# Two small attention products with the high and low parts of one operand side by side

## The chip, the cores and the metric

The kernel runs on one core of one Trainium2 chip, in one launch. The metric is the device time of an execution in microseconds (us), as a median over executions. Lower is better.

## What is computed

A trunk of two layers (`DEPTH = 2`) works on one sequence of 256 positions with 1024 features. A layer is: a gated feed-forward block, attention, a second feed-forward block, and a gated addition of a per-layer embedding. Attention has three branches from one normalised input: a differential attention (branch a), a sparse attention with compressed, selected and windowed keys (branch b) and a sliding-window attention (branch c). The two places that the change touches are these, cut from the reference:

```python
# branch a, diff_attention: 4 heads, 128 values each
attn = pr[:, 0] - lam * pr[:, 1]
o = jnp.einsum('bhqk,bkhe->bqhe', attn, v)            # "values"
o = rms_norm(o, subln_g) * (1.0 - lam_init)
# branch b, nsa_attention: scores against 15 compressed keys per group
s_c = jnp.einsum('bqgrd,bngd->bgrqn', qi, k_cmp) * scale
s_c = s_c + grouped_head_bias(bias_table, dist_c, B_GROUPS, B_REP)
p_c = masked_softmax(s_c, dist_c >= 0)
```

All inputs and outputs are 32-bit floats.

## The kernel before, in words

A matmul on TensorE (PE) takes a stationary operand, which a weight load (PEld) puts in place, and a moving operand that streams through; in this kernel each matmul has its own load. To keep the accuracy of 32-bit floats, each operand is split in two tiles of the type fp32r: a high part (`hi`, made by ScalarE, ACT) and a low part (`lo`, the difference, made by VectorE, DVE). `split` at L225 does it. A product is then three matmuls that add up in one PSUM bank: high times high, high times low, low times high. `mul3` (L234) issues them at L235, L236 and L237. Where `mul3` is called with a stationary pair (xh, xl) and a moving pair (wh, wl), the first two matmuls have the same stationary operand and two moving operands.

The big products (`product`, L305) stream weights from DRAM in pieces of 128x1024 through four `raw` buffers, which ACT (L228) and DVE (L223) split into six pairs of `wh` and `wl`. Names in the profile: `ff` and `fo` are the feed-forward products, `A`, `Ck`, `Cq`, `Bk`, `Bv`, `Bq` the projections of attention, `gate` and `br` the gates and the branch products, `wo` the output product, `pp` and `pg` the embedding's products.

The attention of the three branches runs beside the projections and gates, as side programs (Python generators) that `Flow` steps as the big products go on: `attend_a` from A2 on, `attend_c` from Bk on, `attend_b` after branch a, and `compressed` with `attend_cmp` in a lane of its own. The scheduler of the framework then sets the final order of every engine from dependencies, priorities and a simulated timeline, so the order on each engine is fixed when the kernel is built and each engine works through its own in that order.

Branch a. `attend_a` works on units (m, t): m is a pair of heads, t a block of 128 query rows, four units in a layer. `first` makes the scores `s` (L537, matmuls of 64 rows of the array, two halves of the array in alternation, 12 to a unit) and the softmax. `second` turns the probabilities by transposes (`pt`, L243), splits them (`pT`), and at L626 to L631 multiplies them with the values: the bank `ya` gets, for each head x of the pair and each key block k, a `mul3` whose stationary operands are the probabilities' parts and whose moving operands are 128 columns of the values' high part and low part, `va[0][:, 0, k, hd]` and `va[0][:, 1, k, hd]`. Units with t = 0 have one key block, units with t = 1 have two: 2 x 2 x (1 + 2) = 12 calls in a layer, 24 in all. Then ACT squares `ya` with a sum (L636, twice), DVE (L637) and GpSimd (POOL, L638) make the norm's factor, DVE scales `ya` into `yn` (L639), and PE transposes `yn` (`yt`).

Branch b's compressed keys. `attend_cmp(t)` (L806) forms the scores `sc` of 128 query rows against the compressed keys `kc`: four head pairs j, each a `mul3` with the queries' parts as stationary and 32 columns of `kc`'s high and low part as moving operands (16 calls in all). DVE adds the bias `cbias` (L814), and a softmax and a transpose (`pct`) follow. `own` (L836) later reads the turned result `pcT`.

The bank of `ya` has the tag `y` with one buffer, which `yb` and `yc` use too; the SBUF tiles of tag `stage` have four buffers, shared by the projections' copies, `own`, `rows`, and the norm's squares.

Of the kernel before, what the change touches and what calls it, by code (L numbers as in the profile page):

```python
# [13 lines left out]
AF = mybir.ActivationFunctionType  # L14
ALU = mybir.AluOpType
# [171 lines left out]
def trunk(ctx: ExitStack, tc: tile.TileContext, a: dict, out: bass.AP, index: list):  # L187
    nc = tc.nc
# [7 lines left out]
    def bank(tag, bufs, name):  # L196
        return psum.tile([128, 512], F32, tag=tag, bufs=bufs, name=name)
# [11 lines left out]
    def tp_bank(name):  # L209
        return bank("tp", 3, name)  # L210

    def y_bank(name):
        return bank("y", 1, name)
# [5 lines left out]
    def stage(name="stage"):  # L219
        return base.tile([128, 512], F32, tag="stage", bufs=4, name=name)  # L220
# [13 lines left out]
    def mul3(ps, xh, xl, wh, wl, start, stop):  # L234
        nc.tensor.matmul(ps, xh, wh, start=start, stop=False)  # L235
        nc.tensor.matmul(ps, xh, wl, start=False, stop=False)  # L236
        nc.tensor.matmul(ps, xl, wh, start=False, stop=stop)  # L237
# [266 lines left out]
    def attention(i, norm, after):  # L504
# [21 lines left out]
        def scores(name, q, qb, t, key):  # L526

            ps = [psum.tile([128, 2, 256], F32, tag="s", bufs=2, name=name) for _ in range(2)]
            for m in range(2):
                for x, y in ((0, 0), (0, 1), (1, 0)):  # L530
                    for par in range(2):
                        r = slice(64 * par, 64 * par + 64)
                        kk = key(y, r, m)
                        o = ps[par][:, m, :math.prod(kk.shape[1:])]
                        if len(kk.shape) == 3:
                            o = o.rearrange("p (s n) -> p s n", s=kk.shape[1])
                        nc.tensor.matmul(o, q[r, x, qb[m], t * 128:(t + 1) * 128], kk, start=x + y == 0, stop=x == 1)  # L537
            return ps
# [14 lines left out]
        def turned(blocks):  # L553

            n = len(blocks)
            ps = tp_bank("pt")
            transposes(ps, blocks)
            T = pool.tile([128, 2, 4, 128], F32R, tag="pT", bufs=3, name="pT")
            split(T[:, 0, :n], T[:, 1, :n], ps[:, :n * 128].rearrange("p (j q) -> p j q", q=128))
            return T  # L560
# [11 lines left out]
        def band(first):  # L572
            b = pool.tile([128, 4, 256], F32, tag="band", bufs=2, name="band")
            read_band(b, first)
            return b
# [5 lines left out]
        qk, va, yA = [None] * 2, [None], [None] * NT  # L581
# [16 lines left out]
        def attend_a():  # L598
            bnd = band(0)

            def first(u):
                m, t = u
                nk = 128 * (t + 1)
                s = scores("s", qk[m], [0, 1], t, lambda x, r, k: qk[m][r, x, 2 + k, :nk])
                yield
                p = pool.tile([128, 4, 256], F32, tag="p", bufs=3, name="p")
                st = None
                for st in softmax([p[:, j, :nk] for j in range(4)], [s[j // 2][:, j % 2, :nk] for j in range(4)],
                                  [back(bnd[:, 2 * m + j % 2], nk) for j in range(4)]):
                    yield  # L610
                nc.vector.reciprocal(st[:, 8:12], st[:, 4:8])
                nc.vector.tensor_scalar(st[:, 10:12], st[:, 10:12], nlam[:, i:i + 1], None, op0=ALU.mult)
                for x in range(2):
                    nc.vector.tensor_scalar(p[:, 2 + x, :nk], p[:, 2 + x, :nk], st[:, 10 + x:11 + x], None, op0=ALU.mult)
                    nc.vector.scalar_tensor_tensor(p[:, x, :nk], p[:, x, :nk], st[:, 8 + x:9 + x], p[:, 2 + x, :nk],
                                                   op0=ALU.mult, op1=ALU.add)
                yield
                return p

            def second(u, p):  # L620
                m, t = u
                T = []
                for k in range(t + 1):
                    T.append(turned([p[:, x, k * 128:(k + 1) * 128] for x in range(2)]))
                    yield
                y_ps = y_bank("ya")[:, :256]  # L626
                for x in range(2):
                    o, hd = slice(x * 128, x * 128 + 128), slice((2 * m + x) * 128, (2 * m + x + 1) * 128)
                    for k in range(t + 1):
                        mul3(y_ps[:, o], T[k][:, 0, x, :], T[k][:, 1, x, :], va[0][:, 0, k, hd], va[0][:, 1, k, hd], k == 0, k == t)  # L630
                    yield  # L631
                y = pool.tile([128, 256], F32, tag="yt", bufs=2, name="yn")
                st = pool.tile([128, 32], F32, tag="st", bufs=4, name="st")
                for x in range(2):
                    o = slice(x * 128, x * 128 + 128)
                    nc.scalar.activation(y[:, o], y_ps[:, o], AF.Square, accum_out=st[:, x:x + 1])  # L636
                nc.vector.tensor_scalar(st[:, 2:4], st[:, 0:2], 1.0 / 128, EPS, op0=ALU.mult, op1=ALU.add)  # L637
                nc.gpsimd.tensor_tensor(st[:, 4:6], st[:, 2:4], mhalf[:, :2], op=ALU.pow)  # L638
                nc.vector.tensor_tensor(y.rearrange("p (h e) -> p h e", h=2), y_ps.rearrange("p (h e) -> p h e", h=2),  # L639
                                        st[:, 4:6, None].to_broadcast([128, 2, 128]), op=ALU.mult)  # L640
                yield
                if m == 0:
                    yA[t] = y_tile("yA")
                ps = tp_bank("yt")
                transposes(ps, [y[:, x * 128:x * 128 + 128] for x in range(2)])
                split(yA[t][:, 0, 2 * m:2 * m + 2], yA[t][:, 1, 2 * m:2 * m + 2],
                      ps[:, :256].rearrange("p (k q) -> p k q", k=2), sg[:, i:i + 1])
                yield

            yield from pipelined([(m, t) for m in range(2) for t in range(NT)], first, second)  # L650


        kB, qB, vB, half, sig = [None], [None], [None], [None], [None] * NT
# [54 lines left out]
        kc, vc, c_sb = [None], [None], [None]  # L708
# [96 lines left out]

        def attend_cmp(t):  # L806
            s_ps = tp_bank("sc")
            for j in range(4):
                mul3(s_ps[:, 32 * j:32 * j + 32], qB[0][:, 0, j, t * 128:(t + 1) * 128], qB[0][:, 1, j, t * 128:(t + 1) * 128],
                     kc[0][:, 0, j // 2], kc[0][:, 1, j // 2], True, True)  # L810
            yield
            p = pool.tile([128, 8, 16], F32, tag="pc", bufs=2, name="pc")
            st = pool.tile([128, 32], F32, tag="st", bufs=4, name="st")
            nc.vector.tensor_tensor(p, s_ps[:, :128].rearrange("p (h n) -> p h n", h=8), cbias[:, t], op=ALU.add)  # L814
            nc.vector.tensor_reduce(st[:, 0:8], p, axis=AX.X, op=ALU.max)
            nc.vector.tensor_tensor(p, p, st[:, 0:8, None].to_broadcast([128, 8, 16]), op=ALU.subtract)
            nc.scalar.activation(p, p, AF.Exp)
            yield
            nc.vector.tensor_reduce(st[:, 8:16], p, axis=AX.X, op=ALU.add)
            nc.vector.reciprocal(st[:, 8:16], st[:, 8:16])  # L820
            nc.vector.tensor_tensor(st[:, 0:8].rearrange("p (g a b) -> p g a b", g=2, a=2),
                                    st[:, 8:16].rearrange("p (g a b) -> p g a b", g=2, a=2),
                                    sig[t][:, 0:8].rearrange("p (g b a) -> p g a b", g=2, a=2), op=ALU.mult)
            nc.vector.tensor_tensor(p, p, st[:, 0:8, None].to_broadcast([128, 8, 16]), op=ALU.mult)
            nc.vector.tensor_tensor(p, p, cmask[:, None, t, :].to_broadcast([128, 8, 16]), op=ALU.mult)
            yield
            ps = tp_bank("pct")
            transposes(ps, [p.rearrange("p h n -> p (h n)")])
            pcT[t] = pool.tile([128, 128], F32, tag="pcT", bufs=2, name="pcT")
            nc.scalar.activation(pcT[t], ps[:, :128], AF.Copy)  # L830
            yield
# [257 lines left out]
    h = base.tile([128, NT, D], F32, name="h")  # L1089
# [8 lines left out]
    cbias = base.tile([128, NT, 8, 16], F32, name="cbias")  # L1098
# [10 lines left out]
    def back(b, n, step=1):  # L1109

        return bass.AP(tensor=b.tensor, offset=b.offset + step * (n - 1), ap=list(b.ap)[:-1] + [[-step, n]])
# [65 lines left out]
    for i in range(DEPTH):  # L1177
        n = norms[4 * i:4 * i + 5]
# [68 lines left out]
```

## Time and profile before

| | |
|---|---|
| runs | 1345.94, 1347.99, 1346.43 us |
| median | 1346.43 us |
| the profiled execution's own time | 1346.13 us |
| span of the profiled execution | 1344.3 us, 18242 instructions |
| granted TensorE clock, mean | 0.999 |

| engine | busy us | share of the span | instructions |
|---|---|---|---|
| PE, matmuls | 1326.3 | 99% | 6414 |
| PEld, weight loads | 1093.2 | 81% | 6414 |
| DVE | 945.9 | 70% | 1795 |
| ACT | 783.0 | 58% | 1382 |
| POOL | 20.4 | 2% | 36 |

How to read it: the profile is one execution, and times count from its first instruction. A matmul's row tells when it starts and how long it takes from its start to its modelled end; matmuls overlap, so what one costs in a dense stream is the step from its start to the start of the next one, not its duration. An attention layer takes from about 190 to 470 us and from about 853 to 1133 us.

### The profile page before, as it was taken

How to read it: one execution, taken by the hardware profiler on the slowest of the kernel's cores; microseconds unless marked ns; L12 is line 12 of the kernel's file. 1: busy time of each engine (PE TensorE's matmuls, PEld its weight loads, DVE VectorE, ACT ScalarE, POOL GpSimd, SP SyncE). 2: the span in 40 equal slices, each digit the busy share in tenths (PEclk: the TensorE clock that was granted, in tenths of full speed). 3: DMA queues.
4: the chain of work that ended last, by engine and by line, in shares of the span. 5: the costliest groups of instructions: out<-in, count | busy, mean ns of one | idle time of the engine just before them, and what ended most of it. 6: DMA issues, size and time to landing. Idle time of an engine off the chain costs nothing.

```text
span 1344.3 us, 18242 instructions
## 1 busy us (share of the span) xinstructions
PE 1326.3 (99%) x6414; PEld 1093.2 (81%) x6414; DVE 945.9 (70%) x1795; ACT 783.0 (58%) x1382; POOL 20.4 (2%) x36
## 2 busy tenths in 40 slices
PE   9999999999999999999999999999999999999997
PEld 7778888887887788888888888888888878888886
DVE  6677566768978767665776766577697886767565
ACT  7555455668756555544755545566696656555454
POOL 0000000000000000000000000000000000000000
PEclk9999999999999999999999999999999999999999
DMA  8887665455742578675567875744556425877562
GB/s 302 214 270 220 206 207 187 141 165 168 229 153 79 188 186 237 208 219 184 188 199 216 224 209 186 243 152 162 167 174 207 152 78 177 242 222 214 189 209 78
DMA packets 121993, 257.14 MB, mean 191 GB/s; under 512 B 56944, under 2 KB 62500, under 8 KB 121902
## 3 DMA queue, kind: packets, MB, share of 16 engines
q1 hardware_dynamic: 121150, 254.34, 61.1%
q0 software_dynamic: 320, 1.08, 0.3%
q8 instruction: 50, 0.82, 0.3%
q10 hardware_dynamic: 432, 0.56, 0.1%
q14 instruction: 41, 0.34, 0.1%
HBM read 243.33 MB, written 1.08 MB: 182 GB/s over the span
## 4 chain that ended last, share of the span: by engine, by line
PE 91%; DVE 4%; DMA 2%; ACT 1%; issue 1%; SPq 0%; POOLq 0%; POOL 0%; DVEq 0%; ACTq 0%
PE ff L236 11%; PE ff L237 11%; PE ff L235 11%; PE fo L235 6%; PE fo L236 6%; PE fo L237 6%; PE gate L235 3%; PE gate L237 3%; PE gate L236 3%; PE s L537 2%; PE A L235 2%; PE A L236 2%; PE A L237 2%; DVE wl L223 2%; PE br L236 1%; PE br L235 1%
## 5 line engine op out<-in xcount | busy, mean ns | idle before, releaser
L223 DVE TENSOR_TENSOR wl<-raw,wh 128x1024 fp32r<-128x1024 f32 (+1 forms) x448 | 539.4, 1213 | 174.2 <-ACT wh L228 166.8
L228 ACT ACTIVATE wh<-raw 128x1024 fp32r<-128x1024 f32 (+1 forms) x448 | 468.3, 1050 | 229.0 <-PE fo L237 85.4
L236 PE MATMUL ff<-wl,nT 128*128 128x512 f32 x704 | 273.8, 391 | 1.6 <-DVE wl L223 1.5
L237 PE MATMUL ff<-wh,nT 128*128 128x512 f32 x704 | 272.8, 390 | 0.0
L235 PE MATMUL ff<-wh,nT 128*128 128x512 f32 x704 | 270.9, 391 | 0.3 <-ACT wh L228 0.3
L236 PEld LDWEIGHTS ff<-wl,nT 128*128 128x128 f32 x704 | 132.3, 188 | 30.9 <-DVE wl L223 3.9
L235 PEld LDWEIGHTS ff<-wh,nT 128*128 128x128 f32 x704 | 132.3, 188 | 29.5 <-ACT wh L228 2.1
L237 PEld LDWEIGHTS ff<-wh,nT 128*128 128x128 f32 x704 | 132.3, 188 | 27.3
L236 PE MATMUL fo<-wl,gT 128*128 128x512 f32 x352 | 134.2, 392 | 0.0
L237 PE MATMUL fo<-wh,gT 128*128 128x512 f32 x352 | 133.7, 389 | 0.0
L235 PE MATMUL fo<-wh,gT 128*128 128x512 f32 x352 | 132.5, 389 | 0.0
L474 ACT ACTIVATE act<-ff,stats 128x256 f32<-128x256 f32 x88 | 41.4, 472 | 85.9 <-PE ff L237 85.7
L475 DVE TENSOR_TENSOR gated<-act,ff 128x256 f32<-128x256 f32 x88 | 36.6, 417 | 60.1 <-ACT act L474 60.1
L235 PEld LDWEIGHTS fo<-wh,gT 128*128 128x128 f32 x352 | 66.1, 188 | 13.8
L237 PEld LDWEIGHTS fo<-wh,gT 128*128 128x128 f32 x352 | 66.1, 188 | 13.4
L236 PEld LDWEIGHTS fo<-wl,gT 128*128 128x128 f32 x352 | 66.1, 188 | 13.3
L235 PE MATMUL gate<-wh,nT 128*128 128x512 f32 x192 | 76.3, 399 | 0.0
L237 PE MATMUL gate<-wh,nT 128*128 128x512 f32 x192 | 76.1, 396 | 0.0
L236 PE MATMUL gate<-wl,nT 128*128 128x512 f32 x192 | 75.9, 395 | 0.0
L228 ACT ACTIVATE gT<-whole 128x512 fp32r<-128x512 f32 (+1 forms) x48 | 28.4, 591 | 64.3 <-DVE whole L448 64.2
L548 ACT ACTIVATE p<-p,st 128x128 f32<-128x128 f32 (+1 forms) x128 | 56.8, 445 | 2.9 <-DVE st L546 2.2
L448 DVE COPY whole<-flip 128x512 uint16<-128x512 uint16 (+1 forms) x96 | 38.2, 433 | 14.5 <-DMA flip<-cut 13.9
(301 smaller groups left out, 1997.6 us busy)
## 6 DMA issues: line engine op xcount, KB each, us to landing
raw<-in_wst SPq DMA_DIRECT2D x438, 512.0 KB, 4.4
band<-table SPq DMA_DIRECT2D x10, 512.0 KB, 5.1
raw<-in_wbv SPq DMA_DIRECT2D x4, 420.0 KB, 3.0
flip<-cut SPq DMA_TRANSPOSE x96, 4.1
xt<-in_xt SPq DMA_DIRECT2D x4, 256.0 KB, 5.3
raw<-in_wst SPq DMA_DIRECT2D x4, 256.0 KB, 4.9
h<-in_x SPq DMA_DIRECT2D x2, 512.0 KB, 7.6
band<-table POOLq DMA_DIRECT2D x2, 512.0 KB, 6.9
```

What stands on the lines that cost most here:

```text
L223: nc.vector.tensor_tensor(o, x, y, op=ALU.subtract)
L228: nc.scalar.activation(hi, src, AF.Copy)
L235: nc.tensor.matmul(ps, xh, wh, start=start, stop=False)
L236: nc.tensor.matmul(ps, xh, wl, start=False, stop=False)
L237: nc.tensor.matmul(ps, xl, wh, start=False, stop=stop)
L448: tc.keep_in_program_order(nc.vector.tensor_copy(halves(whole)[:, :128 * m, w], flip[:, w, :m].rearrange("p a b -> p (a b)")))
L474: nc.scalar.activation(act, ps[:, :256], AF.Silu, scale=norm.r(t))
L475: nc.vector.tensor_tensor(held[t][:, 256 * (f % 2):256 * (f % 2) + 256], act, ps[:, 256:], op=ALU.mult)
L537: nc.tensor.matmul(o, q[r, x, qb[m], t * 128:(t + 1) * 128], kk, start=x + y == 0, stop=x == 1)
L548: nc.scalar.activation(p[j], p[j], AF.Exp, bias=st[:, j:j + 1], scale=-1.0, accum_out=st[:, n + j:n + j + 1])
```

## The change

In branch a the first two matmuls of each call become one: the moving operand is 256 columns, the values' high part and, beside it, their low part, and the bank `ya` holds for each head 128 columns of the product with the high part and 128 of the product with the low part. The third matmul (low probabilities, high values) adds to the first half. The two halves are added afterwards: ACT copies the low halves to a `stage` tile (128x256), DVE adds the high halves to it (128x256), and the squares and the scaling that follow read this tile in SBUF in place of the bank.

In `attend_cmp` the same is done with 2 x 32 columns of `kc`; here DVE adds the second half to the scores in one more 128x128 addition.

```diff
-                y_ps = y_bank("ya")[:, :256]
+                y_ps = y_bank("ya").rearrange("p (x v e) -> p x v e", x=2, v=2)
                 for x in range(2):
-                    o, hd = slice(x * 128, x * 128 + 128), slice((2 * m + x) * 128, (2 * m + x + 1) * 128)
+                    hd = slice((2 * m + x) * 128, (2 * m + x + 1) * 128)
                     for k in range(t + 1):
-                        mul3(y_ps[:, o], T[k][:, 0, x, :], T[k][:, 1, x, :], va[0][:, 0, k, hd], va[0][:, 1, k, hd], k == 0, k == t)
+                        nc.tensor.matmul(y_ps[:, x], T[k][:, 0, x, :], va[0][:, :, k, hd], start=k == 0, stop=False)
+                        nc.tensor.matmul(y_ps[:, x, 0], T[k][:, 1, x, :], va[0][:, 0, k, hd], start=False, stop=k == t)
                     yield
                 y = pool.tile([128, 256], F32, tag="yt", bufs=2, name="yn")
+                ys = stage("ya")
                 st = pool.tile([128, 32], F32, tag="st", bufs=4, name="st")
+                nc.scalar.activation(ys[:, 256:].rearrange("p (x e) -> p x e", x=2), y_ps[:, :, 1], AF.Copy)
+                nc.vector.tensor_tensor(ys[:, :256].rearrange("p (x e) -> p x e", x=2), y_ps[:, :, 0],
+                                        ys[:, 256:].rearrange("p (x e) -> p x e", x=2), op=ALU.add)
+                y_ps = ys[:, :256]
...
             s_ps = tp_bank("sc")
+            s_ps = s_ps[:, :256].rearrange("p (x n) -> p x n", x=2)
             for j in range(4):
-                mul3(s_ps[:, 32 * j:32 * j + 32], qB[0][:, 0, j, t * 128:(t + 1) * 128], qB[0][:, 1, j, t * 128:(t + 1) * 128],
-                     kc[0][:, 0, j // 2], kc[0][:, 1, j // 2], True, True)
+                q = [qB[0][:, x, j, t * 128:(t + 1) * 128] for x in range(2)]
+                nc.tensor.matmul(s_ps[:, :, 32 * j:32 * j + 32], q[0], kc[0][:, :, j // 2], start=True, stop=False)
+                nc.tensor.matmul(s_ps[:, 0, 32 * j:32 * j + 32], q[1], kc[0][:, 0, j // 2], start=False, stop=True)
...
-            nc.vector.tensor_tensor(p, s_ps[:, :128].rearrange("p (h n) -> p h n", h=8), cbias[:, t], op=ALU.add)
+            nc.vector.tensor_tensor(p, s_ps[:, 0].rearrange("p (h n) -> p h n", h=8), cbias[:, t], op=ALU.add)
+            nc.vector.tensor_tensor(p, p, s_ps[:, 1].rearrange("p (h n) -> p h n", h=8), op=ALU.add)
```

Since the framework's scheduler sets the order from a simulated timeline, the order of the other attention work moves too. The feed-forward blocks and the output product keep theirs. Counted over the whole program, PE has 40 matmuls less, ACT eight instructions more and DVE twelve. The score matmuls `s` (L537) stand in unbroken runs between other matmuls; there are 54 such runs before and 42 after (27 in each layer before; 22 and 20 after).

First place, PE at the first unit of branch a in the first layer, inside the projection Cq. Before:

```order
L537 MATMUL s<-qkA_1868 128x128 x6
L243 MATMUL qt<-ident,stage 128x128 x2
L235 MATMUL ya<-va,pT 128x128
L236 MATMUL ya<-va,pT 128x128
L537 MATMUL s<-qkA_1868 128x128 x2
L237 MATMUL ya<-va,pT 128x128
L235 MATMUL ya<-va,pT 128x128
L236 MATMUL ya<-va,pT 128x128
L237 MATMUL ya<-va,pT 128x128
L537 MATMUL s<-qkA_1868 128x128 x4
```

After the change, at the same place:

```order
L537 MATMUL s<-qkA_1868 128x128 x6
L243 MATMUL qt<-ident,stage 128x128 x2
L630 MATMUL ya<-va,pT 128x256
L537 MATMUL s<-qkA_1868 128x128 x3
L631 MATMUL ya<-va,pT 128x128
L630 MATMUL ya<-va,pT 128x256
L631 MATMUL ya<-va,pT 128x128
L537 MATMUL s<-qkA_1868 128x128 x3
```

Six matmuls of 128 columns became two of 256 and two of 128; the scores around them are cut at another point.

Second place, PE in the gates of branch a in the first layer, where branch c's scores and values (`yc`) are put between. Before:

```order
L237 MATMUL gate_3014<-wh,nT 128x512
L537 MATMUL s<-kC,qC 128x256 x2
L790 MATMUL yc<-pT,vC 128x512
L537 MATMUL s<-kC,qC 128x256 x4
L235 MATMUL gate_3014<-wh,nT 128x512
L236 MATMUL gate_3014<-wl,nT 128x512
L537 MATMUL s<-kC,qC 128x256 x3
L791 MATMUL yc<-pT,vC 128x512
L537 MATMUL s<-kC,qC 128x256 x3
L237 MATMUL gate_3014<-wh,nT 128x512
```

After, where the first `yc` stands:

```order
L235 MATMUL gate_2881<-wh,nT 128x512
L243 MATMUL qt<-ident,stage 128x128 x4
L796 MATMUL yc<-pT,vC 128x512
L537 MATMUL s<-kC,qC 128x128 x7
L797 MATMUL yc<-pT,vC 128x512
L537 MATMUL s<-kC,qC 128x128 x5
L236 MATMUL gate_2881<-wl,nT 128x512
```

The four short runs of scores that stood here are gone from this place; another unit's twelve scores stand in two runs.

Third place, DVE at the compressed keys' softmax of the first block (`pc` is the softmax's tile, `wl` a weight piece's low part). Before:

```order
L223 TENSOR_TENSOR wl<-raw,wh 128x1024 x3
L814 TENSOR_TENSOR pc<-sc,cbias 128x128
L815 TENSOR_REDUCE st<-pc 128x8
L816 TENSOR_TENSOR pc<-pc,st 128x128
L970 SCALAR_TENSOR_TENSOR th<-th,br_3828 128x512
L819 TENSOR_REDUCE st<-pc 128x8
L971 TENSOR_TENSOR merged_1722<-merged_1722,th 128x512
L820 RECIPROCAL st<-st 128x8
```

After:

```order
L822 TENSOR_TENSOR pc<-sc,cbias 128x128
L223 TENSOR_TENSOR wl<-raw,wh 128x1024
L823 TENSOR_TENSOR pc<-pc,sc 128x128
L824 TENSOR_REDUCE st<-pc 128x8
L825 TENSOR_TENSOR pc<-pc,st 128x128
L223 TENSOR_TENSOR wl<-raw,wh 128x1024
L828 TENSOR_REDUCE st<-pc 128x8
L223 TENSOR_TENSOR wl<-raw,wh 128x1024
L829 RECIPROCAL st<-st 128x8
```

The added addition (L823) follows the first with a weight piece's split between, and three splits that stood ahead of the softmax now stand inside it.

On SP's queue the pieces of weights keep their order; of the reads of the bias bands (L1107) one in each layer is issued two pieces later and one seven pieces earlier. POOL's order is unchanged.

## Rows read from the trace of the kernel before

**Rows 1.** The page: PE's part of the busy times, the granted clock in 40 slices of the span, and the shares of the engines in the chain that ended last.

```profile
PE 1326.3 (99%) x6414; PEld 1093.2 (81%) x6414; DVE 945.9 (70%) x1795; ACT 783.0 (58%) x1382; POOL 20.4 (2%) x36
...
PEclk9999999999999999999999999999999999999999
...
PE 91%; DVE 4%; DMA 2%; ACT 1%; issue 1%; SPq 0%; POOLq 0%; POOL 0%; DVEq 0%; ACTq 0%
```

**Rows 2.** The waits of PE over the whole span: who waited for whom, total us, times, longest.

```profile
PE yb L790 <- DVE yt L800: 1.9, 4, 0.8
PE wo L235 <- ACT mT L231: 1.6, 2, 0.8
...
PE wo L236 <- DVE wl L223: 1.1, 2, 0.6
```

**Rows 3.** Busy time by stretch of the first attention layer: the stretch, its length, then busy us (and instructions) of PE, PEld, DVE, ACT and POOL, the granted clock, the share of the DMA engines and GB/s.

```profile
238.00:300.00 62.00, 62.00 (x353) 52.52 (x352) 41.48 (x99) 39.07 (x96) 2.78 (x4) 1.00 0.47 151
300.00:340.00 40.00, 40.00 (x232) 31.58 (x231) 35.10 (x91) 35.74 (x92) 0.00 (x0) 1.00 0.53 170
340.00:375.00 35.00, 35.00 (x186) 29.42 (x185) 29.03 (x76) 22.51 (x46) 0.00 (x0) 1.00 0.65 212
375.00:404.00 29.00, 29.00 (x149) 24.07 (x148) 24.48 (x63) 17.81 (x36) 0.00 (x0) 1.00 0.52 166
404.00:428.00 24.00, 22.83 (x132) 17.92 (x131) 22.21 (x56) 17.94 (x41) 0.00 (x0) 1.00 0.31 107
```

**Rows 4.** PE in order of time at nine `ya` matmuls in a row, with the neighbours of 512 columns: start us, duration us, engine, line, operation, out<-in, shapes. The rows left out are the six `ya` between.

```profile
260.12 0.39 PE L236 MATMUL Bk<-wl,nT 128*128 128x512 f32 x1
260.35 0.39 PE L237 MATMUL Bk<-wh,nT 128*128 128x512 f32 x1
260.57 0.22 PE L235 MATMUL ya<-va,pT 128*128 128x128 f32 x1
260.63 0.28 PE L236 MATMUL ya<-va,pT 128*128 128x128 f32 x1
...
261.42 0.28 PE L237 MATMUL ya<-va,pT 128*128 128x128 f32 x1
```

**Rows 5.** The same view, the first and the last of fifteen matmuls of 256 columns in a row (projection Ck).

```profile
229.24 0.28 PE L237 MATMUL Ck<-wh,nT 128*128 128x256 f32 x1
...
230.91 0.28 PE L236 MATMUL Ck<-wl,nT 128*128 128x256 f32 x1
```

**Rows 6.** The same view, the first and the last of ten `sc` matmuls of 32 columns in a row.

```profile
378.74 0.26 PE L237 MATMUL sc<-kc,qB 128*128 128x32 f32 x1
...
379.74 0.26 PE L237 MATMUL sc<-kc,qB 128*128 128x32 f32 x1
```

**Rows 7.** The same view, one whole run of twelve score matmuls between gate matmuls.

```profile
396.23 0.40 PE L236 MATMUL gate<-wl,nT 128*128 128x512 f32 x1
396.56 0.98 PE L537 MATMUL s<-kB,qB 64*128 64x256 f32 x12
397.47 0.50 PE L237 MATMUL gate<-wh,nT 128*128 128x512 f32 x1
397.81 0.40 PE L235 MATMUL gate<-wh,nT 128*128 128x512 f32 x1
```

**Rows 8.** The same view, twelve score matmuls in four runs. Left out are, in order, one `yc`, two `gate` and one `yc`, each of 512 columns.

```profile
310.57 0.39 PE L237 MATMUL gate<-wh,nT 128*128 128x512 f32 x1
310.88 0.50 PE L537 MATMUL s<-kC,qC 64*128 64x256 f32 x2
...
311.74 0.74 PE L537 MATMUL s<-kC,qC 64*128 64x256 f32 x4
...
313.06 0.62 PE L537 MATMUL s<-kC,qC 64*128 64x256 f32 x3
...
314.05 0.62 PE L537 MATMUL s<-kC,qC 64*128 64x256 f32 x3
314.59 0.50 PE L237 MATMUL gate<-wh,nT 128*128 128x512 f32 x1
314.93 0.40 PE L235 MATMUL gate<-wh,nT 128*128 128x512 f32 x1
```

**Rows 9.** DVE's groups by line and shape over the whole span: count, busy us, mean ns of one, then idle time before them.

```profile
L223 DVE TENSOR_TENSOR wl<-raw,wh 128x1024 fp32r<-128x1024 f32 x438 | 531.3, 1221 | 171.9 <-ACT wh L228 164.6
...
L639 DVE TENSOR_TENSOR yn<-ya,st 128x256 f32<-128x256 f32 x8 | 3.4, 420 | 3.5 <-POOL st L638 3.5
...
L814 DVE TENSOR_TENSOR pc<-sc,cbias 128x128 f32<-128x128 f32 x4 | 1.1, 286 | 0.0
```

**Rows 10.** ACT's groups in the same form: a copy of 128x256 from PSUM to a `stage` tile.

```profile
L588 ACT ACTIVATE stage<-A,stats 128x256 f32<-128x256 f32 x8 | 3.8, 471 | 2.8 <-PE A L237 2.8
```

**Rows 11.** The chain that ended last, in order of time, at the end of the first attention layer: start us, us, what. The rows left out between are of DVE but for short gaps of issue.

```profile
404.59 0.24 PE gate L237
404.90 1.07 ACT wh L228
405.99 1.23 DVE wl L223
407.22 1.20 DVE own L836 x2
...
426.32 0.68 DVE merged L971
```

## The prediction

> **What bounds the kernel now.** I read the page first: PE is busy for 99% of the span, the granted clock is full in all 40 slices, and 91% of the chain that ended last is PE's [rows 1]. Next the waits: PE waits for others for a few us only, and nearly all of it at the end of the two attention layers, 4.6 us in the three largest groups [rows 2]. Then the stretches of the first attention layer: PE has no idle time from 238 to 404 us, while DVE is idle for 62.00 - 41.48 = 20.5, then 4.9, 6.0 and 4.5 us; only from 404 to 428 us is PE short of work while DVE is full for 22.21 of 24 us [rows 3]. The chain says the same: it runs on PE up to 404.59, passes to ACT and DVE, and comes back after 426 us [rows 11]. So the time is the sum of what PE's instructions cost in its queue, plus a DVE-bound tail of some 22 us in each layer. The question is therefore what 40 matmuls less are worth in PE's queue, and whether the work put on ACT and DVE stays in idle time.
>
> **First edit, `ya`: two matmuls for three.** A matmul of 128 columns steps by (261.42 - 260.63) / 7 = 0.113 us from one start to the next [rows 4]; fifteen of 256 columns step by 1.67 / 14 = 0.119 us [rows 5]. Twice the columns cost 5% more, so below 256 columns something other than the streamed columns sets the step, and taking out one instruction of three is worth nearly a third. A call cost 3 x 0.113 = 0.339 us and will cost 0.119 + 0.113 = 0.232; 24 calls save 24 x 0.107 = **2.6 us**. The new moving operand lies in two pieces; if these streamed as two matmuls do, the saving would be 0. I keep that as the lower end.
>
> The Trainium skill speaks against this edit: TensorE: Matmul & The Clock Gate, in the section Back-to-back issue gap, gives for an isolated stream at full clock a gap of N / 2.4 + 2.5 ns, that is by the streamed columns alone, and by it a call would go from 3 x 56 = 168 to 109 + 56 = 165 ns (estimate from that page), a gain of under 0.1 us over all calls. Rows 4 and 5 don't agree with it; every matmul of this kernel has a load of its own, and for such pairs the same section states 81 ns at 128 columns, also less than the 113 here. The page's section LDWEIGHTS (columns / 1.2 ns, so 107 ns for 128) does fit the 0.111 to 0.119 us of the rows.
>
> **Second edit, `sc`.** Matmuls of 32 columns step by 1.00 / 9 = 0.111 us [rows 6], hardly less than those of 128. So one of 64 columns will cost 0.111 to 0.113, I take 0.111, and each of the 16 calls loses one step: 16 x 0.111 = **1.8 us**; again 0 is the lower end.
>
> **Third, what moves.** The score matmuls use half the array's rows, and a change between them and full matmuls costs PE time. In the whole run the first score starts 0.33 us after its predecessor and the second gate 0.34 us after the first, where 0.23 is the step [rows 4, 7]: 0.10 + 0.11 = 0.21 us at the edges of a run. Twelve scores in one run cost 1.58 - 2 x 0.23 = 1.12 us [rows 7]; in four runs 4.36 - 6 x 0.23 = 2.98 [rows 8], so three more runs cost 1.86, or 0.62 each (pairs of scores are broken there too). The order after has 54 - 42 = 12 runs less. Between 0.21 and 0.62 I take 0.4, about the middle, since the cuts that go away are of both kinds: 12 x 0.4 = **4.8 us**, ends 2.5 and 7.4. This is larger than either edit and no part of its wording; it comes from where the scheduler now puts things.
>
> **What is added.** ACT: eight copies of 128x256 from PSUM, 0.471 us each by the nearest row of that shape [rows 10], 3.8 us. DVE: eight additions of 128x256 at 0.420 and four of 128x128 at 0.286 [rows 9], 3.4 + 1.1 = 4.5 us, 2.25 in a layer. They cost nothing as long as DVE's idle time covers them: 20.5 + 4.9 + 6.0 + 4.5 = 36 us a layer from 238 to 404 [rows 3]. Without that cover they cost 4.5. Behind a `ya` there now stand a copy and an addition ahead of the squares, 0.47 + 0.42 and some 0.1 for the handing over (estimate), 1.0 us more until `yt` can be transposed. In the order after, PE has 20 to 27 matmuls of a projection or gate between the last `ya` of a unit and its `yt`, over 3 us of work; so I cost the longer chain at 0. Without that cover it is 8 x 1.0 = 8 us. The bank `ya` comes free earlier, after the addition. The moved reads of the bias bands land well ahead of their use, since weights pass through SP's queue at the pace at which DVE frees buffers: 0.
>
> **The tail.** The DVE work between the second `own` and the output product is ordered almost as before, with one more weight split in it, 1.2 us [rows 9]. By the order, PE reaches the transposes `pct` that start it earlier than before by more than that, so that the end moves with PE's saving. But a few places get tighter: from the compressed keys to `own`, 64 us that held 10.5 us of DVE idle time [rows 3] get shorter by what PE saves there. For new waits I allow **1.5 us**, between 0 and a doubling of the 4.6 us [rows 2].
>
> **Sum.** -2.6 - 1.8 - 4.8 + 1.5 = -7.7 us. The profiled execution took 1346.13 us, 0.3 under the median of the runs, 1346.43; so 1338.4 on its scale and **1338.7 us** on the median's. No change, for this kernel's measurement, is 0.2% or 2.7 us: 1343.7 to 1349.1.
>
> **The rivals.**
> (a) *Only the runs count*: if streamed columns set the price at `ya` and `sc` (384 before and after, and 96), the edits give 0 and the sum is -4.8 + 1.5 = -3.3: 1343.1 us. Rows 4 to 6 speak against it. 8%. (The gap rule of the Trainium skill's TensorE: Matmul & The Clock Gate, named above, would have it so.)
> (b) *DVE sets the pace of branch b*: from the compressed keys to the tail DVE is busy for 53.5 of 64 us [rows 3]; if PE arrives earlier and only waits for the softmaxes, what the runs save is given back, and -2.6 - 1.8 + 1.5 = -2.9 remains: 1343.5 us. For it: the tail is DVE's already. Against: 10.5 us of idle time. 15%.
> (c) *Runs are dear and nothing new waits*: -2.6 - 1.8 - 7.4 = -11.8: 1334.6 us. 10%.
> (d) *Slower: DVE becomes the bound from the compressed keys to the end of the tail.* It decides from the point where DVE has no idle time from 340 to 404 us. Then what PE saves is all waited away, and the added DVE work lies on the path: +4.5, 1350.9 us. Against: some 5 us of idle time would be left a layer even with PE's saving. 7%.
> (e) *The longer chain from `ya` to `yt` stands open*: +8.0 beside -9.2 + 1.5, so +0.3: 1346.7 us. For it: eight such chains. Against: the distance in the order. 5%.
>
> **How the numbers follow.** The forecast keeps 55%. The range is 1335.0 to 1344.5: it holds the forecast, (a), (b), and the forecast with runs at nearly 0.62, and leaves out (d), (e) and part of (c), under 2 in 10. Faster by over 0.2%: the forecast, (c), and most of (a) and (b), which lie near the bound, 0.55 + 0.10 + 0.05 + 0.09 = 0.79. Within 0.2%: the rest of those two and (e), 0.14. Slower: (d), 0.07.
>
> **What would show it.** PE 6374 matmuls; `ya` of 256 columns stepping by about 0.12 us; a second `sc` step of 0.11; PE's busy time down by 7 to 9 us, with the gain nearly equal in both layers: the first `wo` matmuls about 4 us earlier in the first layer, and about 8 in the second; feed-forward stretches of unchanged length. DVE busy up by about 4.5, ACT by under 4. The prediction is wrong if `ya` of 256 columns steps by 0.22 (the two pieces stream as two), if PE's waits grow by several us at `yt`, `pct` or `mt`, or if the place of the first `wo` doesn't move.

## The result, and the profile after

The changed kernel takes 1366.9 us (median), the kernel before 1347.21 us beside it: 1.0142 times as long, 95% interval 1.0129 to 1.0155, some 19 us slower. The forecast was 1338.7 us; the time lies above the whole range, and above the rival that was to end slower. (One of the four executions of the changed kernel took 1898 us at a mean granted clock of 0.652; the median counts it, the ratio doesn't, and the median of the other three is 1365.46 us.) The profiled execution of the changed kernel took 1365.46 us.

The page first, the lines that answer to [rows 1]:

```profile
PE 1330.4 (98%) x6374; PEld 1096.0 (80%) x6374; DVE 951.4 (70%) x1807; ACT 783.1 (57%) x1390; POOL 20.4 (1%) x36
...
PEclk9999999989999999999999999998999999999999
...
PE 85%; DVE 5%; ACT 3%; DMA 3%; issue 2%; SPq 0%; POOLq 0%; POOL 0%; DVEq 0%; ACTq 0%
```

PE executes 40 matmuls less and is busy for 4 us more. The granted clock, full in all 40 slices before, is lower in two, one in each attention layer; and the chain that ended last runs 6 points less on PE. The added work is small, as forecast: DVE +5.5 us, ACT +0.1.

The waits of PE over the whole span (who waited for whom, total us, times, longest), against [rows 2]:

```profile
PE s L537 <- DVE st L546: 3.7, 2, 1.9
PE ct L243 <- DVE stage L670: 3.5, 1, 3.5
...
PE gate L235 <- ACT stage L701: 1.4, 2, 1.1
...
PE ya L631 <- DVE pT L223: 1.2, 2, 0.8
...
PE Bv L235 <- DVE st L611: 0.9, 2, 0.7
```

None of these was among the waits before; two name the tag `stage`. The stretches of the first attention layer, columns as in [rows 3], say where:

```profile
238.00:300.00 62.00, 54.40 (x284) 45.40 (x283) 37.93 (x89) 32.70 (x82) 2.08 (x3) 0.92 0.37 119
300.00:340.00 40.00, 38.66 (x198) 30.76 (x199) 28.77 (x91) 31.55 (x91) 0.69 (x1) 0.96 0.45 151
340.00:375.00 35.00, 34.11 (x204) 28.02 (x203) 31.76 (x72) 27.02 (x56) 0.00 (x0) 1.00 0.64 210
```

Between 238 and 300 us PE is idle for 7.6 us of 62, at a mean granted clock of 0.92, where it was full; DVE and ACT are busy for *less* than before (37.93 and 32.70 us, against 41.48 and 39.07; the stages start later, so less of the work falls into the stretch). No engine is the bound there: they wait for each other. The stages start later step by step: the projection Bk 0.3 us earlier than before, Bv 4.7 us later, Bq 12.1, the compressed keys 17.7, the first `wo` 14.3; in the second layer the first `wo` is 19.3 us later. The feed-forward stretches keep their length.

One of the places, in order of time (start us, duration us, engine, line, operation, out<-in, shapes; in brackets the idle time before and its releaser). PE:

```profile
262.93 0.33 PE L630 MATMUL ya<-va,pT 128*128 128x256 f32 x1
263.10 0.23 PE L631 MATMUL ya<-va,pT 128*128 128x128 f32 x1
263.16 0.34 PE L630 MATMUL ya<-va,pT 128*128 128x256 f32 x1
263.33 0.22 PE L631 MATMUL ya<-va,pT 128*128 128x128 f32 x1
263.39 0.44 PE L236 MATMUL Bk<-wl,nT 128*128 128x512 f32 x1
...
264.37 0.39 PE L237 MATMUL Bk<-wh,nT 128*128 128x512 f32 x1
266.62 1.63 PE L537 MATMUL s<-kC,qC 64*128 64x128 f32 x12 [1.86 <-DVE st L546]
269.00 0.57 PE L235 MATMUL Bv<-wh,nT 128*128 128x280 f32 x1 [0.75 <-DVE st L611]
```

ACT, at the same time:

```profile
263.80 0.37 ACT L636 ACTIVATE ya<-ya 128x256 f32<-128x256 f32 x1
264.06 0.47 ACT L669 ACTIVATE stage<-Bk,stats 128x256 f32<-128x256 f32 x1
```

and DVE:

```profile
265.07 0.42 DVE L637 TENSOR_TENSOR ya<-ya 128x256 f32<-128x256 f32 x1
265.40 0.48 DVE L670 TENSOR_SCALAR stage<-Bk,stats 128x256 f32<-128x256 f32 x1
265.79 0.41 DVE L546 CUSTOM_DVE_ANT_0 p<-s,band 128x256 f32<-128x256 f32 x1
```

The `ya` matmuls do what was forecast: a pair steps by 263.16 - 262.93 = 0.23 us. But read ACT: the copy of `Bk` out of PSUM (L669) runs at 264.06, directly behind the new copy of `ya` (L636), which can't run before PE has made `ya` at 263.4. In the kernel before, two copies of `Bk` had run by 259.6:

```profile
258.11 0.47 ACT L663 ACTIVATE stage<-Bk,stats 128x256 f32<-128x256 f32 x1 [1.19 <-PE Bk L237]
259.14 0.47 ACT L663 ACTIVATE stage<-Bk,stats 128x256 f32<-128x256 f32 x1 [0.55 <-DVE stage L664]
```

On DVE the other half of the first copy of `Bk` (L670) and then the softmax (L546), for which PE waits at 266.62, stand behind the new addition (L637). A second place, later on PE, with the other kind of loss:

```profile
280.79 0.22 PE L631 MATMUL ya<-va,pT 128*128 128x128 f32 x1
284.50 0.63 PE L243 MATMUL ct<-ident,stage 128*128 128x128 f32 x4 [3.49 <-DVE stage L670]
...
286.35 0.63 PE L237 MATMUL Bq<-wh,nT 128*128 128x512 f32 x1
286.77 0.63 PE L235 MATMUL Bq<-wh,nT 128*128 128x512 f32 x1
...
288.94 0.40 PE L235 MATMUL Bq<-wh,nT 128*128 128x512 f32 x1
289.18 0.39 PE L236 MATMUL Bq<-wl,nT 128*128 128x512 f32 x1
```

PE waits 3.49 us for a copy of `Bk` (L670) whose product PE had finished at 264.6; its ACT part ran at 282.34, again right behind a copy of `ya` (282.07). Then 512 columns step by 286.77 - 286.35 = 0.42 us, at the 1.2 GHz level (granted clock 0.50 from 285.2 to 288.4), and only from 288.9 on by 0.24.

To add this up I take for every matmul of the whole execution the step to the next one, and split it: the step that such a pair of shapes has in the trace before ("PE's steps"); what lies over it while the granted clock is low, waits in these stretches included; what lies over it by more than 0.3 us elsewhere ("waits"); and the small rest. How much falls to the first column depends by 1 to 2 us on the step taken as the normal one.

| us | PE's steps | waits | at the low clock | small rest |
|---|---|---|---|---|
| before | 1275.3 | 12.6 | 0 | 46.5 |
| after | 1268.0 | 26.5 | 14.1 | 45.2 |
| difference | -7.3 | +13.9 | +14.1 | -1.3 |

The sum of the differences is +19.4, that of the two spans too (1363.7 - 1344.3). So the saving came, and waits and the clock took it back almost four times over. Some 4 of the 14.1 us are waits that fell into the stretches at the low clock: with all waits over 0.3 us taken out first, the two columns are about +18 and +10. The mean granted clock allows no more for the second: 0.99 against 0.999, and 0.009 x 1363.7 = 12.3 us.

### The profile page after: what moved, and what is told of

Read it like the earlier page. It is cut to its first block, busy times and chain, and to the rows that moved or that the text cites. A ratio compares the mean times of both kernels' runs of the same rounds, so it can differ in the third digit from the quotient of the medians.

```text
span 1363.7 us, 18172 instructions
## 1 busy us (share of the span) xinstructions
PE 1330.4 (98%) x6374; PEld 1096.0 (80%) x6374; DVE 951.4 (70%) x1807; ACT 783.1 (57%) x1390; POOL 20.4 (1%) x36
## 4 chain that ended last, share of the span: by engine, by line
PE 85%; DVE 5%; ACT 3%; DMA 3%; issue 2%; SPq 0%; POOLq 0%; POOL 0%; DVEq 0%; ACTq 0%
PE ff L235 11%; PE ff L236 11%; PE ff L237 11%; PE fo L236 6%; PE fo L235 6%; PE fo L237 6%; PE gate L235 2%; PE gate L236 2%; PE gate L237 2%; DVE wl L223 2%; DMA raw<-in_wst 2%; PE A L236 2%; PE A L235 2%; PE A L237 2%; PE s L537 2%
## 5 line engine op out<-in xcount | busy, mean ns | idle before, releaser
L448 DVE COPY whole<-flip 128x512 uint16<-128x512 uint16 (+1 forms) x96 | 38.3, 434 | 15.1 <-DMA flip<-cut 14.1
```

What stands on the lines that cost most here:

```text
L448: tc.keep_in_program_order(nc.vector.tensor_copy(halves(whole)[:, :128 * m, w], flip[:, w, :m].rearrange("p a b -> p (a b)")))
```

## The experiments

The theories. **R**: what costs is the buffer that the new copy takes. `stage` has four buffers, which also carry the projections' copies out of PSUM; with `ya` in the ring these copies are held back until PE has made `ya`. **D**: the sum of the two halves costs by itself. **O**: the other order of the tail, which follows `sc`. All times are medians, each beside the kernel before on the same chip.

| label | us | before | ratio, 95% interval |
|---|---|---|---|
| e1_own_tag | 1346.34 | 1346.56 | 0.9995, 0.9987 to 1.0004 |
| e2_before_stage | 1359.09 | 1346.56 | 1.0090, 1.0075 to 1.0105 |
| e3_sc_only | 1350.75 | 1346.56 | 1.0033, 1.0021 to 1.0045 |
| e4_ya_only | 1366.15 | 1346.56 | 1.0142, 1.0129 to 1.0155 |
| e5_own_ya | 1347.12 | 1347.03 | 1.0000, 0.9991 to 1.0009 |
| e6_before_own | 1346.59 | 1347.03 | 0.9995, 0.9986 to 1.0004 |
| e7_noadd_ya | 1342.53 | 1347.03 | 0.9968, 0.9956 to 0.9980 |
| e8_sc_noadd | 1351.03 | 1347.03 | 1.0022, 1.0013 to 1.0031 |
| e9_dead_ya | 1347.94 | 1346.56 | 1.0008, 0.9999 to 1.0017 |
| e10_before_dve | 1347.32 | 1346.95 | 0.9999, 0.9990 to 1.0008 |
| e11_before_dead | 1347.67 | 1346.95 | 1.0009, 0.9998 to 1.0019 |

**Which edit.** e4_ya_only is the edit of `ya` alone, e3_sc_only that of `sc` alone, each exactly as in the change.

> Only the edit at ya, with the sum in the stage ring as in the change; sc as before. Theory R: all of the slowdown is here, 1362 to 1372 us, with the waits of PE at ct and s in the same places. Rival S: 1340 to 1346.

> Only the edit at sc (16 matmuls less, four additions more on DVE), ya as before. Theory R: no part in the slowdown; 1.8 us from the matmuls and two runs of scores less, 1344 us (1342 to 1346.5). Rival S (the additions in the compressed keys' softmax delay pct and the tail): 1348 or more.

`ya` alone gives the whole slowdown. `sc` alone is slower too, by 4 us, where a gain was expected; the two don't add up, since each reorders the rest. Beside the edit of `ya`, that of `sc` changes next to nothing: 1.0142 times the kernel before with it and without it in the change, 0.9995 and 1.0000 in the runs e1_own_tag and e5_own_ya below.

**The buffer.** e1_own_tag is the changed kernel with the sum in a tile of its own tag, and the copied halves in the tile `y` that the unit has anyway:

```diff
-                ys = stage("ya")
+                ys = pool.tile([128, 256], F32, tag="ys", bufs=2, name="ys")
...
-                nc.scalar.activation(ys[:, 256:]..., y_ps[:, :, 1], AF.Copy)
-                nc.vector.tensor_tensor(ys[:, :256]..., y_ps[:, :, 0], ys[:, 256:]..., op=ALU.add)
-                y_ps = ys[:, :256]
+                nc.scalar.activation(y..., y_ps[:, :, 1], AF.Copy)
+                nc.vector.tensor_tensor(ys..., y_ps[:, :, 0], y..., op=ALU.add)
+                y_ps = ys
```

> The changed kernel with the sum of the two halves of ya in two buffers of its own (tag ys, 128x256) and the copy of the low halves in yn's tile, so that nothing of ya stands in the stage ring; same 40 matmuls less, same eight copies and twelve additions. Theory R (the stage ring: its buffers are handed out in program order, so the copies out of PSUM of Bk and Bq queue behind the copy of a ya that PE has not made yet): the waits at ct, s, Bv and gate go, the clock stays full through attention, 1339 us (1335 to 1344). Rival L (the longer chain and the added work on ACT and DVE themselves hold PE up): 1360 to 1368, since chain and work are the same. Rival O (the other order of PE is to blame): 1355 to 1368, since PE's order stays close to that of the changed kernel.

It takes back some 20 us. The same matmuls, copies and additions are executed. ACT in order of time in e1_own_tag:

```profile
258.74 0.47 ACT L669 ACTIVATE stage<-Bk,stats 128x256 f32<-128x256 f32 x1
...
259.76 0.47 ACT L669 ACTIVATE stage<-Bk,stats 128x256 f32<-128x256 f32 x1
...
264.46 0.36 ACT L636 ACTIVATE yn<-ya 128x256 f32<-128x256 f32 x1
```

The copy of `ya` is as late as in the changed kernel, but the first block of `Bk` has left PSUM 5 us before it. e2_before_stage and e6_before_own put the cause on the buffer by itself: the kernel before, with nothing but a copy of `ya` by ACT, which the squares and the scaling then read, in the one in a `stage` tile and in the other in a tile of its own.

```diff
+                ys = stage("ya")                                                  # e2
+                ys = pool.tile([128, 256], F32, tag="ys", bufs=2, name="ys")      # e6
...
+                nc.scalar.activation(ys[:, :256], y_ps, AF.Copy)
+                y_ps = ys[:, :256]
```

> The kernel before with its three matmuls per call and no change at sc; only a copy of ya (128x256, ACT) into a stage tile is added, which the squares and the scaling then read. No addition on DVE. Theory R: the ring alone brings the waits and the lower clock: 1355 to 1370 us, with a wait of PE at ct or Bv of over 1.5 us. Rival L: a copy of 0.4 us eight times and no addition: 1346 to 1350. Rival W (the merged matmuls or their two-piece operands are slow): 1346.

> The kernel before with its three matmuls per call; a copy of ya (128x256, ACT) is added into a buffer of its own. It differs from the run with the same copy into a stage tile (1359.1 us) in the buffer alone. Theory R (the stage ring's order holds up the copies of Bk and Bq): 1346 us (1344 to 1350), with no new wait at ct, qt or yt. Rival L (the copy and the longer chain): 1355 or more.

1359.09 against 1346.59 us, for one instruction a unit that differs in its buffer. ACT in e2_before_stage:

```profile
261.39 0.37 ACT L635 ACTIVATE ya<-ya 128x256 f32<-128x256 f32 x1
261.65 0.47 ACT L666 ACTIVATE stage<-Bk,stats 128x256 f32<-128x256 f32 x1
...
266.46 0.46 ACT L666 ACTIVATE stage<-Bk,stats 128x256 f32<-128x256 f32 x1
```

and in e6_before_own:

```profile
258.36 0.47 ACT L666 ACTIVATE stage<-Bk,stats 128x256 f32<-128x256 f32 x1 [0.90 <-PE Bk L237]
259.39 0.47 ACT L666 ACTIVATE stage<-Bk,stats 128x256 f32<-128x256 f32 x1 [0.55 <-DVE stage L667]
262.27 0.37 ACT L635 ACTIVATE ys<-ya 128x256 f32<-128x256 f32 x1
```

In the ring, the first copy of `Bk` stands behind that of `ya`; out of it, two copies have run by then. The ring also changed the order of the rest: in e2_before_stage the first `yc` of the layer starts 6.8 us earlier than before and Bv 6.2 us later, while in e6_before_own every stage keeps its place to within 0.3 us. So the tile's place in the ring is shown as the cause; whether it holds the copies back by a buffer that isn't free, or by the order that the scheduler made of it, isn't separated, and no run had more buffers in the ring. PE's largest waits in e2_before_stage stand at transposes, `ct` among them as after the change:

```profile
PE yt L243 <- DVE yn L642: 3.6, 2, 1.8
PE qt L243 <- DVE st L612: 3.3, 2, 1.6
PE ct L243 <- DVE stage L667: 2.5, 2, 1.3
```

**What the sum costs without the ring.** e5_own_ya is e1_own_tag without the edit of `sc`. e7_noadd_ya has the merged `ya` matmuls, `sc` as before, and no sum at all: the normalization reads the high halves from PSUM, so that the low part of the values is left out of the result.

```diff
-                ys = stage("ya")
-                nc.scalar.activation(ys[:, 256:]..., y_ps[:, :, 1], AF.Copy)
-                nc.vector.tensor_tensor(ys[:, :256]..., y_ps[:, :, 0], ys[:, 256:]..., op=ALU.add)
-                y_ps = ys[:, :256]
+                y_ps = y_ps[:, :, 0]
```

> The edit at ya alone, its sum in buffers of its own and not in the stage ring; sc as before. Theory A (the ring takes away the whole gain of the edit at ya, and the edit at sc costs 4 us by itself, as it did alone): 1342 us (1340 to 1344). Rival D (the copies and additions for ya cost in new waits what PE saves, whatever buffers they use; sc is not what keeps the gain away): 1345 to 1349.

> Two matmuls for three at ya, with the copies and additions left out (the values' low part is left out of the result); sc as before. 24 matmuls less and nothing added anywhere. If a call costs 0.107 us less (rows of the kernel before) and nothing new waits: 1346.5 - 2.6 = 1343.9 (1342.5 to 1345.5), runs of scores 52 against 54. Rival M (what PE saves is waited away again, since other engines set the pace at the end of attention): 1346 to 1349. Rival T (two pieces stream as two matmuls): 1346.5 and steps of 0.22 us.

PE's saving is real: -4.5 us in e7_noadd_ya. By the split, PE's steps are 2.8 us less (the forecast said 2.6 for `ya`; there are two runs of scores less too), with waits much as before. With the sum, 4.6 us come back (e5_own_ya): D holds for what R leaves, the order that comes with the sum included. e9_dead_ya computes the sum again, into a tile that nobody reads, on top of e7_noadd_ya:

```diff
+                ys = pool.tile([128, 256], F32, tag="ys", bufs=2, name="ys")
+                nc.scalar.activation(ys..., y_ps[:, :, 1], AF.Copy)
+                nc.vector.tensor_tensor(ys..., y_ps[:, :, 0], ys..., op=ALU.add)
```

> The merged ya without its sum (e7_noadd_ya, 1342.5 us), with the eight copies and eight additions put back into a buffer of their own that nobody reads: the squares and the normalization take the high halves straight from PSUM, so the low part of the values is still left out of the result. Theory C (the longer chain from ya to yt is what the sum costs in e5_own_ya): a sum that nobody waits for costs nothing, 1342.5 us, 1341 to 1344.5. Theory W (the additions and copies cost by being on DVE and ACT, or by the order in which the work then stands): as e5_own_ya, 1347, 1345.5 to 1348.5.

5.4 us more than e7_noadd_ya: the longer chain to `yt` (theory C) isn't it. In e9_dead_ya 10 runs of scores less save some 2 us of PE's steps, and waits grow by 7.2 us; among PE's waits are these, which e7_noadd_ya's list doesn't have, at scores and in branch c:

```profile
PE s L537 <- DVE st L546: 1.5, 2, 0.8
...
PE yc L796 <- DVE yt L806: 1.2, 2, 0.6
```

Is it the added DVE work, or the order that comes with it? e10_before_dve and e11_before_dead change no matmul: to the kernel before they add one DVE copy of `ya` into an unread tile (e10), or the ACT copy and a DVE addition (e11), in each unit.

```diff
+                ys = pool.tile([128, 256], F32, tag="ys", bufs=2, name="ys")
+                nc.vector.tensor_copy(ys, y_ps)                          # e10
...
+                nc.scalar.activation(ys, y_ps, AF.Copy)                  # e11
+                nc.vector.tensor_tensor(ys, y_ps, ys, op=ALU.add)        # e11
```

> The kernel before, with one DVE copy of ya (128x256, PSUM to SBUF) added in each of the eight units, into a buffer of its own that nobody reads; no matmul is changed, and the result is whole. In the order as the program is built, the runs of score matmuls fall from 54 to 46, which by the price that e5 against e7 gave (3.1 us of PE's steps for 10 runs) saves 2.5 us. Theory DV (eight more DVE instructions ahead of the squares are what makes softmaxes and yt late, 5 to 7 us of new waits as in e9): 1346.8 - 2.5 + 6 = 1350, 1348 to 1352. Theory OR (the added DVE work costs nothing; in e5 and e9 it is the other order of the calls that waits): 1344.3, 1343 to 1346.5.

> The kernel before, with the ACT copy of ya and one DVE addition of ya to that copy in each of the eight units, in a buffer of its own that nobody reads; no matmul is changed, and the result is whole. 44 runs instead of 54, 3 us by the same price. e6_before_own has shown the ACT copy alone at 0. Theory DV: 1346.8 - 3 + 6 = 1350, 1348 to 1352. Theory OR: 1343.8, 1342.5 to 1346.5. If e10 and e11 differ, it is the addition's wait for ACT's copy on DVE's queue that costs.

Both came out between the two theories, 0 to 1 us above before. In the profile of e11_before_dead PE's steps are 3.6 us less with 10 runs less, and waits 4.5 us more, at a new place:

```profile
PE br L235 <- ACT th L967: 2.3, 2, 1.2
```

So eight more DVE instructions, or the order they bring, do give back what the fewer runs save. Whether it is the work or the order isn't settled: in every variant with more work on DVE the scheduler chose a new order, and none had one without the other.

**`sc`.** e8_sc_noadd is e3_sc_only without the second addition (the low part of the compressed keys is left out of the scores):

```diff
-            nc.vector.tensor_tensor(p, p, s_ps[:, 1]..., op=ALU.add)
```

> The edit at sc alone, with the second addition left out (the compressed keys' low part is left out of the scores); ya as before. Theory S (the additions on DVE in the compressed keys' softmax bring the new waits at pt and yb): 1344.5 (1342.5 to 1346.5). Rival O (the new order of the tail, not the additions): 1348 to 1352, as with the additions.

The median is still 4 us above before, as O had it, but this doesn't clear the additions. Eight of the twelve executions take 1350.4 us or more at a mean granted clock of 0.995 or 0.996; the four others take 1346.7 to 1348.9 us at 0.997 to 0.999. In e3_sc_only five of six take 1350.2 to 1351.0 us at 0.997 to 0.999. So where the clock stays up, the edit without its additions is some 2 to 4 us faster than with them, and most of what its median loses goes with the clock. From the first `sc` of the first layer on, PE's new waits name the softmax side of branch b, in e3_sc_only

```profile
PE pt L243 <- DVE p L875: 2.7, 2, 1.3
```

and in e8_sc_noadd (the profiled execution is a short one, 1347.36 us)

```profile
PE pt L243 <- DVE pT L223: 3.6, 2, 1.8
```

and no wait at `pt` stands in the list of before. So the waits at `pt` come without the additions too. What the additions cost and what the order behind `sc` costs isn't separated: no run had one without the other and the clock alike.

## Why the prediction was wrong

**PE's side came.** The forecast took 2.6 + 1.8 + 4.8 = 9.2 us off PE; by the split, PE's steps and the small rest fell by 7.3 + 1.3 = 8.6. The edit of `ya` was sized right: 0.23 us a pair, 2.8 us in e7_noadd_ya. (By the gap rule of the Trainium skill's TensorE: Matmul & The Clock Gate, section Back-to-back issue gap, the estimate was under 0.1 us; the runs don't agree.) At `sc` a matmul of 64 columns steps by 0.11 us (388.64 to 388.75 in the profile after), as forecast. The runs of scores were somewhat oversized: where 10 went away without another change of the matmuls, they were worth by the split 2.3 us (e9 against e7), 2.7 (e5 against e7, for which the expectation of e10 had 3.1) and 3.6 (e11 against before), 0.23 to 0.36 each and not 0.4, still inside the ends.

**The step that failed** is in "What is added": "They cost nothing as long as DVE's idle time covers them", and with it the allowance of 1.5 us for new waits; PE's waits grew by some 18 us. I priced the copy by its duration and the addition by the idle time of its engine. Engine time was there: in the stretch that lost most, DVE is idle for 24 of 62 us and ACT for 29. What I never asked is what the new tile takes from others, and what stands behind the new instruction on its queue. The tile came from the ring of four `stage` buffers, which the description of the kernel names and the prediction didn't follow: the copies of `Bk` and `Bq` out of PSUM that take the next buffers were put behind a copy that waits for PE's own `ya` (after the change they run at 264.06, 282.34 and 301.39, each directly behind such a copy). The ring is shown by e2 against e6, 12.5 us for one copy a unit, and by e1, some 20 us for the change. (The allowance was also set beside a misread list: the 4.6 us of [rows 2] aren't the three largest groups, since a feed-forward block and the first matmuls of all have waits of 1.5 us each.)

**The clock.** Nothing was set aside for it. Of the 28 us that came on top some 10, and by the mean granted clock at most 12, are PE working at 1.2 GHz after it had waited.

**The longer chain** at 0 stands as far as it was tested: e9_dead_ya has no such chain and is no faster than e5_own_ya. But its neighbour, that the eight copies and additions find room, was wrong by some 4 to 5 us with the order that they bring (e5, e9 against e7), and no rival held it: (d) wanted DVE without idle time from the compressed keys to the tail, and the trace after shows it idle there, for 3.2 of 35 us from 340 to 375.

**The second edit** at -1.8 was wrong in sign where it stood alone, +4.2 us, and worth next to nothing beside the first. I had cited that PE reaches `pct` earlier; in e3_sc_only the first `pct` of the layer starts 3.6 us later than before. So the tail didn't move with PE's saving, which the prediction had taken from the order.

**The rivals.** All took the saving, the added engine time or the chain of `ya` itself as what decides; the one on the slower side, (d), ended at 1350.9. A rival of the form "a buffer shared with another chain makes that chain wait" would have had its point in the code: four buffers, and copies of `Bk` and `Bq` issued while `ya` is still to come.

## What to carry to other kernels

When a change adds a tile, ask from which ring it comes, who takes the next buffers of that ring, and what the new tile itself waits for; a copy of 0.4 us can hold up a projection. Idle time of an engine need not cover an instruction that stands in front of another chain's work in its queue. Where a scheduler sets the order, a saving in PE's queue can be measured by leaving the new dependent work out (here 4.5 us), and it is the difference to the whole edit that must be explained; here no version with the whole result beat the kernel before.

## What the runs showed of the hardware

PE's clock fell to the 1.2 GHz level in the middle of an otherwise full attention layer after waits of a few us in all. In one case a single long wait was enough: in e10_before_dve, whose executions spread from 1345.88 to 1354.29 us, the profiled one (1354.29) shows

```profile
363.88 0.79 PE L235 MATMUL br<-wh,yC 128*128 128x512 f32 x1 [3.32 <-ACT th L966]
...
364.89 0.63 PE L237 MATMUL br<-wh,yC 128*128 128x512 f32 x1
365.32 0.63 PE L235 MATMUL br<-wh,yC 128*128 128x512 f32 x1
...
370.12 0.40 PE L235 MATMUL br<-wh,yC 128*128 128x512 f32 x1
370.35 0.39 PE L236 MATMUL br<-wl,yC 128*128 128x512 f32 x1
```

0.43 us a step (365.32 - 364.89) and then 0.23; the granted clock is 1.00 up to 362.9, 0.50 from 363.0 to 369.6, and 1.00 behind it. Not every wait does it: in e2_before_stage PE had waited 1.82 us up to 266.88 and the granted clock was still 1.00; it was 0.50 from 269.4 on, behind a second wait of 1.64 us that ended at 269.36. So the size of one wait alone doesn't tell.
